# Two-layer encoder trunk on one core: weight loads run further ahead of the weight splits, and the splits queue behind ScalarE's other work

## The chip, the cores and the metric

The kernel runs on one core of a Trainium2 chip. The metric is the device time of one execution in microseconds, the median over several runs. Engines are named as in the profile: PE is TensorE (matmuls and transposes), PEld its weight loads, DVE is VectorE, ACT is ScalarE, POOL is GpSimd, SP is SyncE, which issues nearly all DMAs.

## What is computed

One sequence of 256 tokens with 2048 features passes two layers, all in float32. Each sub-layer is wrapped in RMS norms (one before, one after) and added to the residual `h`:

```python
for layer in range(2):
    hn = rms_norm(h, mix_pre_g[layer])
    y  = even(hn) if layer == 0 else odd(hn)      # attention, then its output projection
    h  = h + rms_norm(y, mix_post_g[layer])
    c  = memory_cross_attention(rms_norm(h, mem_pre_g[layer]), rms_norm(mem, mem_norm_g[layer]), wq, wk, wv, wo)
    h  = h + rms_norm(c, mem_post_g[layer])
    f  = relu(rms_norm(h, mlp_pre_g[layer]) @ w_up) ** 2 @ w_down     # 2048 -> 8192 -> 2048
    h  = h + rms_norm(f, mlp_post_g[layer])
```

`even` is 8 heads of 2-D neighbourhood attention and 8 heads of sliding-window attention with sinks; `odd` is differential attention with 8 heads of 256. Memory attention has 4 heads over 256 memory tokens.

## The kernel before

**Arithmetic.** Every float32 operand is split into a high and a low part in the `fp32r` format, and a product is three matmuls, high x high, high x low and low x high (`mm3`, line 257; the up projection of the MLP has its own loop, lines 721 and 725, where one matmul takes a high weight with both parts of the activation). PE therefore needs each weight in two parts, `w[:, 0]` and `w[:, 1]`.

**Weight units.** A unit is 256 rows by 512 columns of a weight matrix: 512 KB in HBM. `Weights.load` does all that a unit needs, at once in program order. SP issues the DMA into a raw buffer (line 180; three raw buffers). ACT writes the high part, DVE the low part. For input projections, where the norm's gain is folded in, these are two ACT instructions (line 193) and two DVE instructions (line 194) of 128x512; for output projections one of each, 128x1024 (lines 188 and 189). Nine buffers hold split units (`NW`); a few units use a buffer of another tile instead and may be loaded only when that is free (`gate`). PE asks for unit j by `W.get(j)`, and that call lets all units up to j + 4 be loaded (`AHEAD`). All units of the program stand in one list, in the order of use.

**Order of the work.** PE's order is written by hand: `manual_schedule` takes PE's instructions as the program issues them, and a small calendar (`Line`: `later`, `when`, `tick`, `until`) puts transposes and attention matmuls between the weight matmuls. ACT, DVE, POOL and SP are ordered by the compiler's scheduler, which follows the program order as a priority and takes what is ready. Each engine then runs its list strictly in order.

**The places that the prediction speaks of.** Blocks are 512 columns of a projection: 8 units, 96 matmuls of 128x512.

- `qs0` and `qs1`, the two blocks of sliding-window queries near the start. `evac_T` scales a finished block into a tile `q` on ACT (line 427), applies the rotary embedding on DVE (lines 412 to 415), has PE transpose it, and splits it into `qT` on ACT and DVE (lines 398 and 399).
- The memory queries (`mq`) and values (`mv`) in `mem_and_mlp`: `qT` is split in the same way, between units of `mv` and `mo`; the memory features `mt` come from DRAM and are split into `xT` (lines 340 and 341).
- The end of a sub-layer, `Leave` (lines 361 to 393). It takes the output projection in chunks of 512 columns, in the order token tile 0, chunks 0 to 3, then token tile 1. For each chunk DVE adds the matmul result into `y` (line 307), ACT takes the sum of squares (`junk`, line 321), DVE multiplies by the gain (line 375); after chunk 3 DVE forms `rb` (line 383), POOL takes the inverse root `rr` (line 325) and DVE updates the four blocks of `h` (line 388). PE transposes these blocks (line 348) between later matmuls, and ACT and DVE split them into `xT`.
- An MLP group is 512 of the 8192 hidden columns: 96 matmuls of the down projection of one group (line 257), then the up projection of a later one (lines 721 and 725). `split_u` brings its result out: `ue` on ACT (line 679), `s` on DVE, square and relu on ACT, then the split into `lt` (lines 398 and 399).

Of the kernel before, what the change touches and what calls it, by code (L numbers as in the profile page):

```python
# [3 lines left out]

# [1 line left out]

# [23 lines left out]
NW = 9  # L30
# [7 lines left out]
D_TRS, D_RMS, D_EVM, D_EVU, M_TR, M_GO = 4, 13, 11, 6, 11, 1  # L38
A_ROPE, A_NA, M_AT = 10, 1, 8
A_DF, DF_GAP, DF_T, DF_M, DF_O = 6, 5, 7, 4, 8  # L40
AHEAD = 4
L_MQ, L_MV, L_UP, L_Q = 6, 5, 8, 6
START = (2, 6, "AAAaABaBabbraBBabababbbab")
G_MIX, G_MEM, G_MLP, G_MN = 0, 2, 4, 6
# [27 lines left out]
def trunk(  # L72
# [3 lines left out]
    mlp_w_up, mlp_w_down, out,  # L76
):
    nc = tc.nc
    V, A, G, PE = nc.vector, nc.scalar, nc.gpsimd, nc.tensor
# [18 lines left out]
    gains = keep.tile([P, P], F32, name="gains")  # L98
# [24 lines left out]
    class Line:  # L123
        def __init__(self):
            self.now, self.q, self.n = 0, [], 0
# [21 lines left out]
        def until(self, done):  # L147
            while not done():
                self.now, _, fn = heapq.heappop(self.q)
                fn()  # L150

    line = Line()


    class Weights:
        def __init__(self):
            self.specs, self.tiles, self.n, self.wait, self.open = [], {}, 0, [], set()
            self.goal, self.live = -1, 0

        def plan_in(self, src, n0, g, spare=(), gate=None):  # L160

# [12 lines left out]
                    self.specs.append((src, k0 + 2 * kp, n * 512, None, None, None))  # L174
            return a

        def load(self, j):
            src, k0, n0, tag, _, g = self.specs[j]
            raw = rawp.tile([P, 2, 512], F32, tag="raw", name="raw")
            nc.sync.dma_start(  # L180
                raw, src[k0 * P : (k0 + 2) * P, n0 : n0 + 512].rearrange("(k p) n -> p k n", p=P)
            )
            if tag is None:
                w = wp.tile([P, 2, 2, 512], F32R, tag="w", name="w")
            else:
                w = sb.tile([P, 2, 2, 512], F32R, tag=tag, bufs=1, name="w")
            if g is None:
                A.copy(w[:, 0], raw)  # L188
                V.tensor_tensor(w[:, 1], raw, w[:, 0].bitcast(F32), ALU.subtract)  # L189
            else:  # L190
                for kk in range(2):
                    gk = gains[:, g * KT + k0 + kk : g * KT + k0 + kk + 1]
                    A.activation(w[:, 0, kk], raw[:, kk], AF.Copy, scale=gk)  # L193
                    V.scalar_tensor_tensor(  # L194
                        w[:, 1, kk], raw[:, kk], gk, w[:, 0, kk].bitcast(F32), ALU.mult, ALU.subtract
                    )
            self.tiles[j] = w

        def pump(self):
            while self.n < min(self.goal + 1, len(self.specs)):  # L200
                _, _, _, tag, g, _ = self.specs[self.n]
                if g is None or g in self.open:
                    if tag is None:
                        if self.live == NW:
                            return
                        self.live += 1
                    self.load(self.n)
                else:
                    self.wait.append(self.n)
                self.n += 1  # L210

        def upto(self, j):
            self.goal = max(self.goal, j)
            self.pump()

        def free(self, gate):

            self.open.add(gate)
            for j in self.wait:
                self.load(j)  # L220
            self.wait = []

        def get(self, j):
            self.upto(j + AHEAD)
            return self.tiles[j]

        def done(self, j):

            if self.specs[j][3] is not None:
                return  # L230

            self.live -= 1
            self.pump()

    W = Weights()
# [418 lines left out]
    def mem_and_mlp(l, R, kT, nxt):  # L654
# [31 lines left out]
        def up(g):  # L686
# [42 lines left out]
            for b in range(2):  # L729
                split_u(ut, 2 * b, pts[2 * b : 2 * b + 2])  # L730
# [4 lines left out]
        for g in range(NG):  # L735
# [249 lines left out]
```

## Time and profile before

| | us |
|---|---|
| median of 3 runs | 2377.68 (2373.12 to 2378.13) |
| the profiled execution's own time | 2374.78 |
| its span, first to last instruction | 2372.7 |
| PE busy in it | 2346.2 (99%) |
| DVE busy | 1611.9 (68%) |
| ACT busy | 1377.7 (58%) |
| mean DMA rate | 190 GB/s |
| mean granted TensorE clock | 0.998 of full speed |

The profiled execution took 2.1 us more than its span, for what lies before the first and after the last instruction, and it was 2.9 us under the median of the runs. Times in the trace count from the span's start. In the rows below, the idle time in brackets is that of the engine just before the instruction, with what ended it.

### The profile page before, as it was taken

The page shows a single profiled execution, that of the slowest core. Times are in us where ns is not written, and L with a number is a line of the kernel's source. Part 1 is how long each engine was busy: PE and PEld are TensorE (multiplying, and loading weights), DVE is VectorE, ACT ScalarE, POOL GpSimd, SP SyncE. Part 2 cuts the span into 40 slices and gives each one's busy share as a digit, 9 for nine tenths or more (in the row PEclk, how much of TensorE's full clock was granted, in tenths as well). Part 3 has the DMA queues.
Part 4 walks back from the last instruction along what each step waited for, and adds up shares of the span by engine and source line. Part 5 has one row for each costly group of instructions (what it writes and reads, how often), then busy time and mean ns, then how long its engine had stood idle before and what let it go on. Part 6 is the DMA issues. An engine that isn't in the chain of part 4 may idle for free.

```text
span 2372.7 us, 32033 instructions
## 1 busy us (share of the span) xinstructions
PE 2346.2 (99%) x11687; PEld 1984.9 (84%) x11687; DVE 1611.9 (68%) x2545; ACT 1377.7 (58%) x2280; POOL 28.0 (1%) x46
## 2 busy tenths in 40 slices
PE   8999999999999999999999999999999999999998
PEld 7788887888888888888888888887888888888887
DVE  6776678856666656666876667788666666666666
ACT  6756567765545545545665655577655545555553
POOL 0000000000000000000000000000000000000000
PEclk9999999999999999999999999999999999999999
DMA  7657655565655666665565555655666665665663
GB/s 250 212 183 233 188 193 190 178 209 181 198 193 183 195 196 183 195 197 187 180 195 172 171 188 169 204 178 181 202 195 194 187 195 187 188 199 182 196 195 114
DMA packets 238279, 451.88 MB, mean 190 GB/s; under 512 B 21289, under 2 KB 22185, under 8 KB 237353
## 3 DMA queue, kind: packets, MB, share of 16 engines
q1 hardware_dynamic: 237832, 449.32, 59.7%
q8 instruction: 91, 1.49, 0.3%
q14 instruction: 68, 0.55, 0.1%
q10 hardware_dynamic: 288, 0.52, 0.1%
HBM read 445.59 MB, written 5.15 MB: 190 GB/s over the span
## 4 chain that ended last, share of the span: by engine, by line
PE 91%; DMA 3%; DVE 3%; ACT 2%; issue 1%; POOL 0%; SPq 0%; DVEq 0%; POOLq 0%; ACTq 0%
PE mm L257 59%; PE at L721 14%; PE at L725 7%; PE mm L721 5%; PE mm L725 2%; PE at L257 2%; DVE w L194 1%; DMA raw<-in_even_w_in 1%; PE tr L435 1%; DMA raw<-in_odd_w_in 1%; PE tr L348 1%; ACT w L193 1%; PE at L505 0%; DMA h<-in_x 0%; ACT junk L321 0%
## 5 line engine op out<-in xcount | busy, mean ns | idle before, releaser
L257 PE MATMUL mm<-w,lt 128*128 128x512 f32 x4032 | 926.9, 390 | 0.0
L257 PEld LDWEIGHTS mm<-w,lt 128*128 128x128 f32 x4032 | 754.8, 188 | 155.9
L194 DVE SCALAR_TENSOR_TENSOR w<-raw,gains,w 128x512 fp32r<-128x512 f32 x944 | 678.2, 747 | 261.5 <-ACT w L193 258.7
L193 ACT ACTIVATE w<-raw,gains 128x512 fp32r<-128x512 f32 x944 | 636.0, 717 | 354.1 <-PE mm L257 268.9
L257 PE MATMUL mm<-w,xT 128*128 128x512 f32 x2784 | 674.0, 395 | 2.0 <-DVE v L403 1.1
L189 DVE TENSOR_TENSOR w<-raw,w 128x1024 fp32r<-128x1024 f32 x336 | 411.2, 1224 | 377.6 <-ACT w L188 376.8
L188 ACT CAST w<-raw 128x1024 fp32r<-128x1024 f32 x336 | 353.1, 1051 | 439.1 <-PE mm L725 193.3
L257 PEld LDWEIGHTS mm<-w,xT 128*128 128x128 f32 x2784 | 513.2, 189 | 104.4 <-DVE v L403 1.9
L721 PE MATMUL at<-xT,w 128*128 128x512 f32 x1440 | 368.8, 391 | 0.0
L721 PEld LDWEIGHTS at<-xT,w 128*128 128x128 f32 x1440 | 262.7, 188 | 49.0
L725 PE MATMUL at<-xT,w 128*128 128x256 f32 x1440 | 211.0, 283 | 0.0
L725 PEld LDWEIGHTS at<-xT,w 128*128 128x128 f32 x1440 | 197.2, 191 | 9.4
L312 DVE TENSOR_TENSOR y<-mm,y 128x512 f32<-128x512 f32 x256 | 175.5, 685 | 15.6 <-PE mm L257 15.4
L721 PE MATMUL mm<-xT,w 128*128 128x512 f32 x480 | 147.8, 389 | 0.0
L721 PEld LDWEIGHTS mm<-xT,w 128*128 128x128 f32 x480 | 90.1, 188 | 19.3
L725 PE MATMUL mm<-xT,w 128*128 128x256 f32 x480 | 96.7, 283 | 0.0
L725 PEld LDWEIGHTS mm<-xT,w 128*128 128x128 f32 x480 | 74.9, 192 | 0.0
L679 ACT COPY ue<-at 128x256 f32<-128x256 f32 x90 | 33.7, 374 | 28.0 <-DVE s L680 13.9
L399 DVE TENSOR_TENSOR lt<-s,lt 128x512 fp32r<-128x512 f32 x64 | 44.1, 689 | 3.6 <-ACT lt L398 3.6
L257 PEld LDWEIGHTS at<-kT,qT 128*128 128x128 f32 x240 | 34.5, 191 | 10.5 <-ACT qT L398 4.2
L257 PE MATMUL at<-kT,qT 128*128 128x256 f32 x240 | 37.3, 288 | 5.8 <-ACT qT L398 3.4
L321 ACT ACTIVATE junk<-y 128x512 bf16<-128x512 f32 x32 | 20.1, 629 | 38.5 <-DVE y L307 38.3
(113 smaller groups left out, 1063.6 us busy)
## 6 DMA issues: line engine op xcount, KB each, us to landing
raw<-in_mlp_w_up SPq DMA_DIRECT2D x256, 512.0 KB, 4.1
raw<-in_mlp_w_down SPq DMA_DIRECT2D x256, 512.0 KB, 4.2
raw<-in_odd_w_in SPq DMA_DIRECT2D x96, 512.0 KB, 4.2
raw<-in_even_w_in SPq DMA_DIRECT2D x72, 512.0 KB, 4.3
raw<-in_even_w_out SPq DMA_DIRECT2D x32, 512.0 KB, 4.2
raw<-in_odd_w_out SPq DMA_DIRECT2D x32, 512.0 KB, 3.8
mt<-memT SPq DMA_DIRECT2D x32, 256.0 KB, 4.0
raw<-in_mem_wk SPq DMA_DIRECT2D x16, 512.0 KB, 4.4
```

Source lines behind the costliest of these rows:

```text
L188: A.copy(w[:, 0], raw)
L189: V.tensor_tensor(w[:, 1], raw, w[:, 0].bitcast(F32), ALU.subtract)
L193: A.activation(w[:, 0, kk], raw[:, kk], AF.Copy, scale=gk)
L194: V.scalar_tensor_tensor(w[:, 1, kk], raw[:, kk], gk, w[:, 0, kk].bitcast(F32), ALU.mult, ALU.subtract)
L257: PE.matmul(pt, lhs(a), rhs(b), start=first and i == 0, stop=last and i == 2)
L312: V.tensor_tensor(ysl, pt, ysl, ALU.add)
L348: PE.transpose(pt[:, i * P : (i + 1) * P], h[:, t, k * P : (k + 1) * P], ident)
L399: V.tensor_tensor(lo, src, hi.bitcast(F32), ALU.subtract)
L435: PE.transpose(tp[:, i * P : (i + 1) * P], u[:, i * P : (i + 1) * P], ident)
L679: A.copy(e, pt[:, S:])
L721: PE.matmul(pts[nt], wn, both, start=kp + kk == 0, stop=kp == 7 and kk == 1)
L725: PE.matmul(pts[nt][:, :S], wn, both[:, :S], start=False, stop=False)
```

## The change

`Weights.load` is cut in two. `fetch(j)` takes a raw buffer and issues the DMA; `split()` takes the oldest raw buffer and issues the ACT and DVE instructions. `W.get(j)` now lets units up to j + 6 be fetched and units up to j + 4 be split, and there are four raw buffers in place of three. A small class `Urgent` stands in for ACT and notes the last instruction that anything but a weight split has issued there. The splits are issued under `tc.issue_after(A.last)`: each ACT instruction of a split gets an edge that keeps it behind that noted instruction in ACT's list. Units that wait for a gate go to a list `shut`, and when the gate opens to `late`, from which they are fetched first. The tile `ue` shares two buffers with `q` instead of having its own two, which makes room for the fourth raw buffer. The matmuls and their order are as before.

```diff
-AHEAD = 4
+AHEAD, FETCH, NRAW = 4, 2, 4
-    rawp = ctx.enter_context(tc.tile_pool(name="rawp", bufs=3))
+    rawp = ctx.enter_context(tc.tile_pool(name="rawp", bufs=NRAW))
+    class Urgent:
+        def __init__(self):
+            self.last = None
+        def activation(self, *a, **k):
+            self.last = nc.scalar.activation(*a, **k).ins
+        def copy(self, *a, **k):
+            self.last = nc.scalar.copy(*a, **k).ins
+    A = Urgent()
...
-        def load(self, j):
-            src, k0, n0, tag, _, g = self.specs[j]
+        def fetch(self, j):
+            src, k0, n0 = self.specs[j][:3]
             raw = rawp.tile([P, 2, 512], F32, tag="raw", name="raw")
             nc.sync.dma_start(
                 raw, src[k0 * P : (k0 + 2) * P, n0 : n0 + 512].rearrange("(k p) n -> p k n", p=P)
             )
+            self.raws.append((j, raw))
+
+        def split(self):
+            j, raw = self.raws.pop(0)
...
-            if g is None:
-                A.copy(w[:, 0], raw)
...
+            with tc.issue_after(A.last) if A.last is not None else nullcontext():
+                if g is None:
+                    nc.scalar.copy(w[:, 0], raw)
+                    V.tensor_tensor(w[:, 1], raw, w[:, 0].bitcast(F32), ALU.subtract)
+                else:
+                    for kk in range(2):
+                        gk = gains[:, g * KT + k0 + kk : g * KT + k0 + kk + 1]
+                        nc.scalar.activation(w[:, 0, kk], raw[:, kk], AF.Copy, scale=gk)
...
         def pump(self):
...
+            while True:
+                j = self.next()
+                if j < min(self.fetch_goal + 1, len(self.specs)) and len(self.raws) < NRAW:
+                    self.fetch(j)
...
+                elif self.raws and self.raws[0][0] <= self.split_goal and (
+                    self.live < NW or self.specs[self.raws[0][0]][3] is not None
+                ):
+                    self.split()
                 else:
-                    self.wait.append(self.n)
-                self.n += 1
+                    return
...
         def get(self, j):
-            self.upto(j + AHEAD)
+            self.upto(j + AHEAD, FETCH)
             return self.tiles[j]
...
-                e = sb.tile([P, S], F32, tag="ue", bufs=2, name="ue")
+                e = sb.tile([P, S], F32, tag="q", bufs=2, name="ue")
```

PE's list and POOL's list hold the same instructions in the same order before and after. The lists of ACT, DVE and SP are in another order; three places follow. Line numbers of the changed kernel lie some 17 to 35 higher than those of the kernel before: L162 and L165 are the noted ACT instructions, L210 and L215 the splits on ACT, L216 those on DVE.

ACT at the end of block `qs0`, before (`q_570` and `q_579` bring out the two halves of `qs0`; the `w` are weight units of `qs1`, of which `w_532` and `w_551` are the third and fourth):

```order
L193 ACTIVATE w_532<-raw_530,gains_88 128x512 x2
L193 ACTIVATE w_551<-raw_549,gains_88 128x512 x2
L427 ACTIVATE q_570<-mm_404,rs_568 128x512
L193 ACTIVATE w_591<-raw_589,gains_88 128x512 x2
L427 ACTIVATE q_579<-mm_418,rs_577 128x512
L193 ACTIVATE w_611<-raw_609,gains_88 128x512 x2
L193 ACTIVATE w_637<-raw_635,gains_88 128x512 x2
L398 CAST qT_403<-tr_628 128x512
```

The same place now (the first unit of `qs1` is `w_498`):

```order
L162 ACTIVATE q_574<-mm_408,rs_572 128x512
L162 ACTIVATE q_583<-mm_422,rs_581 128x512
L215 ACTIVATE w_498<-raw_453,gains_88 128x512 x2
L215 ACTIVATE w_517<-raw_477,gains_88 128x512 x2
L215 ACTIVATE w_536<-raw_496,gains_88 128x512 x2
L215 ACTIVATE w_555<-raw_515,gains_88 128x512 x2
L215 ACTIVATE w_595<-raw_534,gains_88 128x512 x2
L215 ACTIVATE w_615<-raw_553,gains_88 128x512 x2
L165 CAST qT_407<-tr_632 128x512
```

Both `q` of `qs0` now stand ahead of all splits for `qs1`; before, the first four units of `qs1` were split ahead of them.

DVE at the end of the MLP of layer 0, `Leave`, before (the matmul results `mm_10021`, `mm_10061` and `mm_10078` are the last chunk of token tile 0 and the first two of token tile 1):

```order
L307 TENSOR_TENSOR y_83<-mm_10021,y_83 128x512
L375 TENSOR_TENSOR y3_10051<-y_83,g_9928 128x512
L383 TENSOR_SCALAR rb_10053<-ssl_9930,part_9932 128x1
L388 SCALAR_TENSOR_TENSOR h_82<-y_83,rr_10055,h_82 128x512 x3
L388 SCALAR_TENSOR_TENSOR h_82<-y3_10051,rr_10055,h_82 128x512
L307 TENSOR_TENSOR y_83<-mm_10061,y_83 128x512
L194 SCALAR_TENSOR_TENSOR w_10179<-raw_10177,gains_88,w_10179 128x512
L307 TENSOR_TENSOR y_83<-mm_10078,y_83 128x512
```

The same place now (`mm_10025`, `mm_10065` and `mm_10082` are the same three chunks):

```order
L342 TENSOR_TENSOR y_83<-mm_10025,y_83 128x512
L342 TENSOR_TENSOR y_83<-mm_10065,y_83 128x512
L410 TENSOR_TENSOR y3_10055<-y_83,g_9932 128x512
L418 TENSOR_SCALAR rb_10057<-ssl_9934,part_9936 128x1
L342 TENSOR_TENSOR y_83<-mm_10082,y_83 128x512
L423 SCALAR_TENSOR_TENSOR h_82<-y_83,rr_10059,h_82 128x512 x3
L423 SCALAR_TENSOR_TENSOR h_82<-y3_10055,rr_10059,h_82 128x512
```

The four updates of `h` stood ahead of the next two chunks' additions; now they stand behind both.

ACT at the second half of the memory queries in layer 1, before (`qT_13928<-tr_14264` is the split that the attention scores wait for):

```order
L193 ACTIVATE w_14236<-raw_14234,gains_88 128x512 x2
L188 CAST w_14249<-raw_14247 128x1024
L340 CAST xT_84<-mt_14189 128x4x128
L398 CAST qT_13928<-tr_14264 128x512
L487 ACTIVATE p_14278,s_14283<-at_14271,nm_14281 128x256 x2
```

The same place now:

```order
L215 ACTIVATE w_14227<-raw_14199,gains_88 128x512 x2
L215 ACTIVATE w_14240<-raw_14212,gains_88 128x512 x2
L165 CAST qT_13932<-tr_14270 128x512
L210 CAST w_14253<-raw_14225 128x1024
L162 ACTIVATE p_14284,s_14289<-at_14277,nm_14287 128x256 x2
```

The 128x1024 split of the first unit of `mo` and a split of `mt` stood ahead of `qT`; now `qT` stands ahead of that unit, and the `mt` splits are done earlier. In layer 0 the corresponding unit `w_3777` still stands ahead of `qT`.

## Rows read from the trace of the kernel before

**Rows 1.** The page, part 1: busy time, share of the span, instructions

```profile
PE 2346.2 (99%) x11687; PEld 1984.9 (84%) x11687; DVE 1611.9 (68%) x2545; ACT 1377.7 (58%) x2280; POOL 28.0 (1%) x46
```

**Rows 2.** Two consecutive MLP groups: busy time, granted clock, DMA

```profile
762.49:806.52 44.03, 44.03 (x225) 37.70 (x225) 28.61 (x39) 23.42 (x35) 0.00 (x0) 1.00 0.62 191
806.52:850.55 44.03, 44.03 (x225) 37.70 (x225) 28.60 (x39) 23.41 (x35) 0.00 (x0) 1.00 0.61 191
```

**Rows 3.** Wait view of PE: us in total, times, longest us

```profile
PE at L257 <- ACT qT L398: 3.4, 3, 1.7
PE at L257 <- DVE qT L399: 2.4, 3, 1.0
...
PE mm L257 <- ACT q L427: 0.9, 1, 0.9
PE at L257 <- DVE pT L399: 0.9, 1, 0.9
PE at L257 <- DVE lt L399: 0.8, 2, 0.4
```

**Rows 4.** Timeline, end of block qs0: start, duration, engine, line, instruction

```profile
60.06 0.67 ACT L427 ACTIVATE q<-mm,rs 128x512 f32<-128x512 f32 x1
...
60.78 4.40 PE L257 MATMUL mm<-w,xT 128*128 128x512 f32 x18 [0.87 <-ACT q L427]
...
60.92 0.22 DVE L412 TENSOR_TENSOR rope<-q,cst 128x64 f32<-128x64 f32 x1
...
61.52 0.74 DVE L194 SCALAR_TENSOR_TENSOR w<-raw,gains,w 128x512 fp32r<-128x512 f32 x1
```

**Rows 5.** Timeline of DVE, end of the MLP of layer 0

```profile
1150.05 0.21 DVE L383 TENSOR_SCALAR rb<-ssl,part 128x1 f32<-128x1 f32 x1
1150.92 2.74 DVE L388 SCALAR_TENSOR_TENSOR h<-y,rr,h 128x512 f32<-128x512 f32 x4 [0.66 <-POOL rr L325]
...
1154.84 0.68 DVE L307 TENSOR_TENSOR y<-mm,y 128x512 f32<-128x512 f32 x1
1155.44 0.68 DVE L375 TENSOR_TENSOR y<-y,g 128x512 f32<-128x512 f32 x1
```

**Rows 6.** The page, part 5: busy us, mean ns, idle before

```profile
L193 ACT ACTIVATE w<-raw,gains 128x512 fp32r<-128x512 f32 x944 | 636.0, 717 | 354.1 <-PE mm L257 268.9
...
L679 ACT COPY ue<-at 128x256 f32<-128x256 f32 x90 | 33.7, 374 | 28.0 <-DVE s L680 13.9
...
L321 ACT ACTIVATE junk<-y 128x512 bf16<-128x512 f32 x32 | 20.1, 629 | 38.5 <-DVE y L307 38.3
```

**Rows 7.** Timeline of PE and POOL, memory queries of layer 0

```profile
369.53 0.60 PE L348 MATMUL tr<-cst,h 128*128 128x128 f32 x4
...
372.74 0.60 PE L348 MATMUL tr<-cst,h 128*128 128x128 f32 x4
...
370.08 0.99 POOL L325 TENSOR_TENSOR rr<-rb,mhalf 128x1 f32<-128x1 f32 x1 [13.01 <-DVE rb L383]
```

**Rows 8.** Timeline at qT in layer 0, and the window around it

```profile
400.18 1.05 ACT L188 CAST w<-raw 128x1024 fp32r<-128x1024 f32 x1 [1.95 <-DMA raw<-in_mem_wo]
...
402.28 0.51 PE L257 MATMUL at<-kT,qT 128*128 128x256 f32 x2 [1.66 <-ACT qT L398]
...
400.00:409.00 9.00, 6.39 (x27) 5.16 (x26) 5.33 (x11) 4.78 (x11) 0.00 (x0) 0.81 0.44 155
```

**Rows 9.** Timeline at qT in layer 1, and the window around it

```profile
1609.85 0.50 PE L257 MATMUL at<-kT,qT 128*128 128x256 f32 x2 [1.28 <-ACT qT L398]
...
1609.00:1618.00 9.00, 7.20 (x37) 6.09 (x38) 7.20 (x16) 4.83 (x12) 0.00 (x0) 1.00 0.51 164
```

**Rows 10.** DMA issues, first 130 us: count, KB each, us to landing

```profile
bias<-scr SPq DMA_DIRECT2D x4, 96.0 KB, 4.6
```

**Rows 11.** Timeline of one MLP group, PE and ACT

```profile
762.33 21.92 PE L257 MATMUL mm<-w,lt 128*128 128x512 f32 x96
...
767.60 0.60 ACT L398 CAST lt<-s 128x512 fp32r<-128x512 f32 x1
```

More of the change, by code (lines that the diff above doesn't have):

```diff
@@ L2 @@
 import math
-from contextlib import ExitStack
+from contextlib import ExitStack, nullcontext
 import numpy as np
@@ L78, in trunk @@
     nc = tc.nc
-    V, A, G, PE = nc.vector, nc.scalar, nc.gpsimd, nc.tensor
+    V, G, PE = nc.vector, nc.gpsimd, nc.tensor
     keep = ctx.enter_context(tc.tile_pool(name="keep", bufs=1))
@@ L152, in trunk @@
     line = Line()
+    class Urgent:
[6 more added lines that the diff above has]
+    A = Urgent()
     class Weights:
         def __init__(self):
-            self.specs, self.tiles, self.n, self.wait, self.open = [], {}, 0, [], set()
-            self.goal, self.live = -1, 0
+            self.specs, self.tiles, self.n, self.open = [], {}, 0, set()
+            self.shut, self.late, self.raws = [], [], []
+            self.fetch_goal, self.split_goal, self.live = -1, -1, 0
         def plan_in(self, src, n0, g, spare=(), gate=None):
@@ L182, in load @@
             )
+            self.raws.append((j, raw))
+        def split(self):
+            j, raw = self.raws.pop(0)
+            _, k0, _, tag, _, g = self.specs[j]
             if tag is None:
+                self.live += 1
                 w = wp.tile([P, 2, 2, 512], F32R, tag="w", name="w")
@@ L186, in load @@
                 w = sb.tile([P, 2, 2, 512], F32R, tag=tag, bufs=1, name="w")
-            if g is None:
-                A.copy(w[:, 0], raw)
[L189 to L196, printed above, removed]
@@ L197, in load @@
-            self.tiles[j] = w
-        def pump(self):
[L200 to L207, printed above, removed]
-                else:
-                    self.wait.append(self.n)
-                self.n += 1
@@ L212, in upto @@
-        def upto(self, j):
-            self.goal = max(self.goal, j)
+            with tc.issue_after(A.last) if A.last is not None else nullcontext():
[6 more added lines that the diff above has]
+                        nc.scalar.activation(w[:, 0, kk], raw[:, kk], AF.Copy, scale=gk)
+                        V.scalar_tensor_tensor(
+                            w[:, 1, kk], raw[:, kk], gk, w[:, 0, kk].bitcast(F32), ALU.mult, ALU.subtract
+                        )
@@ new lines, in split, with next @@
+            self.tiles[j] = w
+        def next(self):
+            if self.late:
+                return self.late[0]
+            while self.n < len(self.specs):
+                g = self.specs[self.n][4]
+                if g is None or g in self.open:
+                    return self.n
+                self.shut.append(self.n)
+                self.n += 1
+            return len(self.specs)
+        def pump(self):
+            while True:
+                j = self.next()
+                if j < min(self.fetch_goal + 1, len(self.specs)) and len(self.raws) < NRAW:
+                    self.fetch(j)
+                    if self.late:
+                        self.late.pop(0)
+                    else:
+                        self.n += 1
+                elif self.raws and self.raws[0][0] <= self.split_goal and (
+                    self.live < NW or self.specs[self.raws[0][0]][3] is not None
+                ):
+                    self.split()
+                else:
+                    return
@@ L214, in upto @@
+        def upto(self, j, more=0):
+            self.split_goal = max(self.split_goal, j)
+            self.fetch_goal = max(self.fetch_goal, j + more)
             self.pump()
@@ L218, in free @@
             self.open.add(gate)
-            for j in self.wait:
-                self.load(j)
-            self.wait = []
+            self.late, self.shut = self.late + self.shut, []
+            self.pump()
         def get(self, j):
-            self.upto(j + AHEAD)
+            self.upto(j + AHEAD, FETCH)
             return self.tiles[j]
         def done(self, j):
-            if self.specs[j][3] is not None:
-                return
-            self.live -= 1
+            if self.specs[j][3] is None:
+                self.live -= 1
             self.pump()
```

## The prediction

> **What bounds the kernel now.** I read the busy times first. PE is busy 99% of the span, no other engine over 70% except PE's own weight loads, 84% [rows 1]. Then one stage at a time, since a mean hides stages. The MLP is 32 groups and well over half of the span; two neighbouring groups take 44.03 us each, the same to the hundredth, with PE busy for all of it [rows 2]. A stage in which PE never stands has nothing to give to a change that only brings weights or results earlier. So the change can matter only where PE waits, and the wait view lists these places: `qT` on ACT 3.4 us and on DVE 2.4, `q` 0.9, `pT` 0.9, `lt` 0.8 [rows 3]. That is 8.4 us in all, in some ten places in the attention parts, and PE waits for no weight unit. What PE waits for is a result that stands in ACT's or DVE's list behind a weight split. This caps the gain at about 8 us, or 0.35%, before any new wait. About 0.2%, or 4.75 us, is what a measurement of this kernel can tell from no change.
>
> PE's order is unchanged, so each place can be judged alone: how long is the chain of ACT and DVE work from one matmul to the next one that needs its result, and how many matmuls cover it? The cover is counted at 21.92 us for 96 matmuls, 0.228 us each [rows 11].
>
> **What goes.**
>
> 1. *`qT` in layer 0.* ACT waited 1.95 us for a DMA from `mem_wo`, split that unit for 1.05 us from 400.18, and only then came `qT`; PE stood 1.66 us for its high part [rows 8], and up to 1.0 for the low part [rows 3]. The unit still stands ahead of `qT` in the new list, but its DMA is let go two units earlier. At most the wait of 1.95 goes, and at least nothing, since four other units now crowd ahead of it. I take half, -1.0.
> 2. *`qT` in layer 1.* PE stood 1.28 us [rows 9] and again up to 1.0 [rows 3]. The 128x1024 split now follows `qT`. Its 1.05 us [rows 8] and part of the `mt` split that stood there go; the cast and low part of `qT` itself still take longer than the three matmuls before them. -1.3, between -1.0 and -1.6.
> 3. *`pT`* near 92 us, -0.9, and the two waits for `lt`, -0.6 of 0.8 [rows 3]: each result stood behind one 128x1024 split that is now behind it.
> 4. The third pair of waits for `qT`, some 1.2 us near 68 us, stays: twelve split instructions now stand ahead of it, as the order of ACT at `qs0` shows. 0.
>
> Sum of what goes: -3.8.
>
> **What comes.** Here I walk through the new lists.
>
> 1. *First unit of `qs1`.* Its split is now behind both `q`. From the end of the last matmul of `qs0`: hand-over 0.1, `q` 0.67, four rotary steps that hold DVE from 60.92 to 61.52, 0.6, then the low part of the unit, 0.74 [rows 4]: 2.1 us. One matmul of 0.2 runs on the high part alone, so PE stands 1.9 us. The old wait of 0.87 for `q` [rows 4] goes. Net +1.0, between 0 (units split sooner than I read) and +1.9.
> 2. *End of the MLP of layer 0.* The first update of `h` now stands behind the addition that waits for the very last matmul before the transposes of `h`. An addition holds DVE 0.60 us (1154.84 to 1155.44), an update a quarter of 2.74, 0.69 [rows 5]. With 0.1 of hand-over PE stands 1.4. Before it did not, the updates began at 1150.92 and ended ahead of that matmul's result. +1.4, between 0 and +1.6.
> 3. *End of `o3` in layer 1.* The same order with one chunk between: 12 matmuls cover 2.7 us. Behind the addition stand two multiplications, so 3 x 0.60, small steps 0.2, half a weight unit 0.74, `rb` to the first `h` 0.87, and the update 0.69 [rows 4, 5]: 4.3. +1.6, between 0 and +2.2.
> 4. *End of `oa1` in layer 0.* The same, but lighter: 0.60 twice, 0.87, 0.69 and hand-overs, 2.9 against 2.7. +0.2, up to +0.8.
> 5. *Memory queries of layer 0.* The fifth unit's low part now stands on DVE behind all four updates of `h` of token tile 1, and these behind a sum of squares that stands on ACT behind an `mt` split. Chain: that split about 0.6 and `junk` 0.63 [rows 6], `rb` to `h` 0.87, updates 2.74 [rows 5], low part 0.74 [rows 4], 5.6 us. Cover: PE's period of four transposes and twelve matmuls is 3.21 us (369.53 to 372.74) [rows 7], and four more transposes and two matmuls add 0.8: 4.0. +1.6. POOL took 0.99 here [rows 7], a little more than 0.66 of idle time in rows 5, so up to +2.2; at least 0.
> 6. *SP's queue.* The loads of the attention bias now stand behind raw fetches that wait for a buffer. They take 4.6 us to land [rows 10], and an addition on DVE ahead of the second softmax waits for the first of them. I find about 1 us of lateness with other work behind it, and take +0.4, between 0 and +2.
> 7. The rest is nothing, by its cover. In an MLP group the second four units of the down projection are now split after `lt`. `lt` ended at 768.20, 5.9 us after the group's first matmul, with gain splits between its steps that now come later; a split of 1.05 on ACT and about 1.3 on DVE (twice half a unit) would end at 8.2. The fifth unit is needed after 48 matmuls, at 10.9 [rows 4, 8, 11]. The margin is 2.7 us; if it were gone, each group would pay what is missing. The fourth raw buffer adds no instruction; `ue` keeps two buffers.
>
> Sum of what comes: 1.0 + 1.4 + 1.6 + 0.2 + 1.6 + 0.4 = +6.2. Net +6.2 - 3.8 = +2.4. On the profiled execution's 2374.78 us that is 2377.2. The runs' median lies 2.9 higher, at 2377.68, so I forecast **2380.0**, no change that can be told.
>
> **Rivals.**
>
> - *Gains alone.* The scheduler's list is only an order; if DVE reaches the updates of `h` with time to spare, the new waits shrink to little and the old ones go. All of what goes, the clock in layer 0 with it (see below), is -3.8 - 1.7 = -5.5; with 0.5 of new waits, 2372.7, at the best 8.4 + 1.7 less, 2367.6. For it: PE's waits in rows 3 do stand behind splits. Against: the orders printed above, where the work ahead of `h` is counted. Chance 0.17, of which 0.14 falls below 2372.9.
> - *The clock falls at the new waits* (slower). After PE's waits at 402 us the granted clock averaged 0.81 over 400 to 409 [rows 8]: part of that stretch ran at the lower level, 1.2 GHz, the rest at 2.4. That is at most 0.19 x 9 = 1.7 us. After the waits at 1610 it stayed at 1.00 [rows 9]. Ahead of the fall PE had stood 1.66 us and then up to 1.0; where it held, 1.28 and up to 1.0. My new waits of 1.9, 1.4, 1.6 and 1.6 us are like the one place as much as like the other. If each of the four is like the first and costs 1.7 us, +6.8: 2380.0 + 6.8 = 2386.8; two of them are enough for over 0.2%. Chance 0.17. The Trainium skill's page "TensorE: Matmul & The Clock Gate", section "HAM oscillation — how this bites in real kernels", says that a long enough stop between bursts of matmuls sends the next burst off at the lower clock, and that this is paid at every such stop. The row at 402 agrees, the row at 1610 shows a stop that was not long enough.
> - *The MLP margin is less than I count* (slower). Thirty of the groups bring `ue` out, 90 copies at three each [rows 6]. For each us beyond the margin of 2.7 the kernel takes 30 us more, 2410. Rows 11 speak against it. Chance 0.04.
> - *PE is not at its limit.* If matmuls could follow each other more closely once their data is early, the weight loads' 84% [rows 1] would be the measure, and 0.16 x 2373 = 380 us would be open; a fiftieth of it would be -7.6, 2370. Two groups of exactly 44.03 us with no wait in them [rows 2] say that nothing is open there. Chance 0.02. This is the rule of the Trainium skill's page "Perfetto Trace Analysis", section "Identifying the Most-Contended Engine": the busy share of matmuls is a poor measure of headroom, the busy share of weight loads a better one. The repeated 44.03 disagrees with it here.
>
> **How the numbers follow.** My own case has 0.60: from 2373.9 (the new waits at their lower bounds, -3.8) to 2384.6 (all at their upper ones, 10.7 - 3.8 = +6.9); 0.50 of it lies within 0.2% of the median, 0.10 above. Faster: 0.14 + 0.02 = 0.16. Slower: 0.10 + 0.17 + 0.04 = 0.31. Same: 0.50 + 0.03 = 0.53. The range reaches into the gains and takes in the clock: 2370.5 to 2389.0. It leaves out the MLP, and the far ends of the gains and of the clock.
>
> **What would show it.** Right: waits of 1 to 2 us for DVE `h` at transposes near 1153 and 1565 us, for a weight unit near 61 and 374 us, and no wait for `pT` near 92; ACT no longer idle for `mem_wo` near 400; an MLP group still at 44.03. Wrong: no wait at transposes of `h` (gains alone), a clock under 1.00 after the new waits, or a group longer than 44.1.

## The result and the profile after

The changed kernel took 2396.14 us, the median of 4 runs (2393.26 to 2399.3). The kernel before, run on the same chip, took 2375.72 (4 runs). The ratio is 1.0086, 95% interval [1.0067, 1.0106]. That is 20.4 us more, where 2380.0 with a range of 2370.5 to 2389.0 was forecast. The profiled execution took 2397.52 us, span 2395.7, against 2374.78 and 2372.7 before: the span grew by 23.0 us.

The page's first part, for the changed kernel:

```profile
PE 2355.3 (98%) x11687; PEld 1989.8 (83%) x11687; DVE 1595.7 (67%) x2545; ACT 1362.0 (57%) x2280; POOL 27.8 (1%) x46
```

No instruction was added [rows 1]. PE has 9.1 us more of busy time for the same matmuls, and the other 13.9 us of the 23.0 are time in which it stands. ACT and DVE show some 16 us less of busy time each, but they do not work faster: a gain split takes 716 ns on ACT where it took 717 [rows 6]. The busy time counts the overlap of neighbouring instructions once (944 gain splits of 717 ns are 677 us, and [rows 6] has 636.0 us), so less of it means that they stand closer together, in bunches. The wait view of PE says for what it stands (us in total, times, longest):

```profile
PE tr L383 <- DVE h L423: 5.8, 3, 2.9
PE at L610 <- DMA graw<-in_mem_norm_g: 5.7, 1, 5.7
PE at L292 <- ACT qT L165: 4.8, 4, 2.2
PE mm L292 <- ACT w L215: 4.0, 2, 2.6
PE mm L292 <- DVE w L216: 2.6, 4, 1.6
PE tr L733 <- ACT junk L162: 2.6, 2, 1.4
PE at L292 <- DVE qT L434: 1.7, 4, 0.6
```

The row with `graw` is the start of the program and was there before. Without the waits for a DMA at the start, all rows of this view, the smaller ones too, sum to 24.4 us, those of before to 10.4. So 14.0 us are waits. There are three new kinds: for `h`, for weight units (`w`), and at the transposes of `u` (L733), which stand behind `junk` on ACT at the start of the MLP. The old ones for `qT` grew in sum, from 5.8 to 6.5 us: near 68 us and in layer 0 they grew, in layer 1 they shrank from 2.24 to 0.54.

The remainder, PE's longer busy time, is mostly TensorE's clock. The window view gives busy time of PE, PEld, DVE, ACT, POOL, then the granted clock, the DMA share and GB/s:

```profile
60.00:80.00 20.00, 16.23 (x69) 12.50 (x70) 15.57 (x33) 11.54 (x22) 0.00 (x0) 0.91 0.64 200
409.00:420.00 11.00, 8.17 (x27) 6.62 (x27) 7.06 (x15) 4.50 (x11) 0.00 (x0) 0.69 0.56 196
720.00:764.00 44.00, 44.00 (x226) 37.67 (x225) 28.19 (x38) 23.43 (x34) 0.00 (x0) 1.00 0.57 192
1166.00:1176.00 10.00, 9.60 (x36) 7.78 (x37) 6.55 (x13) 2.14 (x6) 0.00 (x0) 0.68 0.11 40
1620.00:1635.00 15.00, 11.75 (x50) 8.90 (x49) 10.55 (x16) 9.24 (x15) 0.00 (x0) 0.89 0.56 191
```

In the four stretches outside the MLP the clock is at its full level of 2.4 GHz for a part only and at 1.2 GHz for the rest. A missing 0.31 of 11 us is at most 3.4 us, 0.32 of 10 is 3.2, 0.11 of 15 is 1.7 and 0.09 of 20 is 1.8: at most 10.1 us, where in the kernel before I found one such stretch, with at most 1.7 [rows 8]. With the waits, 14.0 + 8.4 = 22.4 of 23.0 us. The window in the MLP shows PE busy for all of it at full clock, as in [rows 2]: nothing changed there.

**The largest wait**, at the end of the MLP of layer 0. The timeline of the changed kernel (start, duration, engine, line, instruction; in brackets the idle time before it):

```profile
1157.72 5.83 PE L292 MATMUL mm<-w,lt 128*128 128x512 f32 x25
1160.15 0.74 DVE L216 SCALAR_TENSOR_TENSOR w<-raw,gains,w 128x512 fp32r<-128x512 f32 x1
...
1160.94 2.07 DVE L216 SCALAR_TENSOR_TENSOR w<-raw,gains,w 128x512 fp32r<-128x512 f32 x3
1162.92 1.28 DVE L342 TENSOR_TENSOR y<-mm,y 128x512 f32<-128x512 f32 x2
...
1164.84 0.69 DVE L342 TENSOR_TENSOR y<-mm,y 128x512 f32<-128x512 f32 x1
...
1165.59 2.74 DVE L423 SCALAR_TENSOR_TENSOR h<-y,rr,h 128x512 f32<-128x512 f32 x4
...
1166.40 1.11 PE L383 MATMUL tr<-cst,h 128*128 128x128 f32 x4 [2.85 <-DVE h L423]
```

Four low parts of the next block's weights hold DVE from 1160.15 to 1162.92. Only then come two additions, and a third at 1164.84, for the last matmul before the transposes; PE had ended that matmul at 1163.55. The updates of `h` stand behind all three. In [rows 5] `rb` and `h` stood first. The weights that went ahead here are not needed by the transposes that PE stands at.

**A wait of the edge's own making**, at the memory values of layer 1:

```profile
1619.74 1.27 ACT L165 CAST xT<-mt 128x512 fp32r<-128x512 f32 x2 [1.30 <-DMA mt<-memT]
...
1624.00 0.62 ACT L165 CAST xT<-mt 128x512 fp32r<-128x512 f32 x1 [2.41 <-DMA mt<-memT]
...
1624.97 0.62 ACT L165 CAST xT<-mt 128x512 fp32r<-128x512 f32 x1 [0.36 <-DMA mt<-memT]
1625.50 5.01 ACT L215 ACTIVATE w<-raw,gains 128x512 fp32r<-128x512 f32 x8
...
1626.27 0.64 PE L292 MATMUL mm<-w,xT 128*128 128x512 f32 x1 [2.56 <-ACT w L215]
```

ACT stands 2.41 us and again 0.36 for `mt`, and behind it stand eight split instructions which PE needs. The edge has put them behind the casts of `mt`, so ACT may not do them while it waits.

### The profile page after: what moved, and what is told of

It reads as the page before. It is cut to its first block, busy times and chain, and to the rows that moved or that the text cites. A ratio compares the mean times of both kernels' runs of the same rounds, so it can differ in the third digit from the quotient of the medians.

```text
span 2395.7 us, 31841 instructions
## 1 busy us (share of the span) xinstructions
PE 2355.3 (98%) x11687; PEld 1989.8 (83%) x11687; DVE 1595.7 (67%) x2545; ACT 1362.0 (57%) x2280; POOL 27.8 (1%) x46
## 4 chain that ended last, share of the span: by engine, by line
PE 88%; DVE 5%; DMA 3%; ACT 2%; issue 1%; POOL 0%; SPq 0%; DVEq 0%; POOLq 0%; ACTq 0%
PE mm L292 56%; PE at L756 14%; PE at L760 7%; PE mm L756 5%; PE mm L760 2%; PE at L292 2%; DVE w L216 2%; DMA mt<-memT 1%; ACT w L215 1%; DVE xT L376 1%; DVE h L423 1%; PE tr L470 1%; ACT junk L162 1%; PE at L540 0%; DMA h<-in_x 0%
## 5 line engine op out<-in xcount | busy, mean ns | idle before, releaser
L216 DVE SCALAR_TENSOR_TENSOR w<-raw,gains,w 128x512 fp32r<-128x512 f32 x944 | 660.1, 748 | 109.3 <-ACT w L215 106.2
L215 ACT ACTIVATE w<-raw,gains 128x512 fp32r<-128x512 f32 x944 | 620.2, 716 | 191.6 <-DMA raw<-in_mlp_w_up 136.9
L211 DVE TENSOR_TENSOR w<-raw,w 128x1024 fp32r<-128x1024 f32 x336 | 403.6, 1222 | 116.5 <-ACT w L210 114.1
L210 ACT CAST w<-raw 128x1024 fp32r<-128x1024 f32 x336 | 341.3, 1049 | 128.5 <-DMA raw<-in_mlp_w_down 92.4
L715 DVE TENSOR_TENSOR s<-at,ue 128x256 f32<-128x256 f32 x90 | 38.3, 425 | 297.9 <-ACT ue L165 295.7
L165 ACT COPY ue<-at 128x256 f32<-128x256 f32 x90 | 33.6, 373 | 326.6 <-PE at L756 321.3
L162 ACT ACTIVATE s<-s 128x512 f32<-128x512 f32 x120 | 74.6, 632 | 0.9
```

The source lines that it names most:

```text
L162: self.last = nc.scalar.activation(*a, **k).ins
L165: self.last = nc.scalar.copy(*a, **k).ins
L210: nc.scalar.copy(w[:, 0], raw)
L215: nc.scalar.activation(w[:, 0, kk], raw[:, kk], AF.Copy, scale=gk)
L216: V.scalar_tensor_tensor(w[:, 1, kk], raw[:, kk], gk, w[:, 0, kk].bitcast(F32), ALU.mult, ALU.subtract)
```

## The experiments

Each kernel was compared with the kernel before on the same chip (2374.7 to 2375.7 us, its medians), and each profile quoted is of one execution. In the expectations, E names the edge as the cause (E1 at the `mt` casts, E2 at the ends of sub-layers), F the longer queue of fetches on SP, L the lateness of the splits, G the place in the list that the fourth buffer gives to splits, and H its rival. What a text says beside a letter goes before this list.

### Which part of the change

**e1**, the changed kernel without its edge:

```diff
-            with tc.issue_after(A.last) if A.last is not None else nullcontext():
+            with nullcontext():
```

> The changed kernel with the edge taken out: splits are issued without issue_after, the rest of the change (fetch six ahead, four raw buffers, ue in the buffers of q) stays. Theory E (the edge makes the loss: splits wait in ACT's list for work that itself waits, and reach DVE in a bunch ahead of the updates of h): 2374 to 2379 us, the waits for h near 1166 and for a weight unit near 1626 gone. Theory F (the deeper fetch makes it: SP's list holds other loads behind raw fetches that wait for a buffer): 2390 to 2397, the wait near 1626 stays.

2381.66 us, ratio 1.0025 [1.0016, 1.0035], 2.7 above the range of theory E and far from F; both waits that it named are gone. The edge makes 14.5 of the 20.4 us. Six are left.

**e2**, the edge alone: `AHEAD, FETCH, NRAW = 4, 0, 3`, and `ue` with its own two buffers.

> The changed kernel with the edge alone: fetch and split both four ahead, three raw buffers, ue with buffers of its own. Theory E: 2390 to 2398 us, with the waits for h at the ends of the sub-layers as in the changed kernel. Theory F: 2374 to 2380, those waits gone.

2408.34 us, 1.0138 [1.0124, 1.0152], above both ranges. The edge costs 33 us with three raw buffers; the earlier fetch and the fourth buffer, which cost 6 without it, give 12 back with it. The parts do not add. (This kernel also has `load` cut in two. That was not run with three buffers and no edge; with four, e1 has it and e3 has not, and they lie 0.5 us apart.) The wait view of PE has more of the same kind:

```profile
PE tr L383 <- DVE h L423: 12.3, 5, 6.1
```

ACT's wait view shows one thing more, here for the changed kernel and for e2:

```profile
ACT w L215 <- DMA raw<-in_mlp_w_up: 136.9, 145, 2.3
ACT w L215 <- DMA raw<-in_mlp_w_up: 193.8, 189, 3.4
```

In the kernel before ACT stood 43.8 us for these loads, in e1 1.7. A unit whose split is held back keeps its raw buffer, so the next load is issued later, and ACT then stands for it. With three buffers in place of four there is less to take this up, which fits the 12 us; no run separates it from the order on DVE. In the MLP itself PE does not stand for it.

**e3**, the kernel before with a fourth raw buffer and nothing else (`bufs=4`, `ue` in `q`'s buffers to make room).

> The kernel before with a fourth raw buffer and ue in the buffers of q, nothing else. Both theories: within 3 us of the kernel before, 2373 to 2379. If the fourth buffer alone lets ACT reach the splits at qT sooner, the waits for qT near 402 and 1610 shrink and it is 2371 to 2374.

2381.20 us, 1.0024 [1.0013, 1.0035]: the six us of e1 come with the buffer alone. A buffer that adds no instruction was expected to be free. Its two largest waits of PE are those of e1 too (3.5 and 3.0 us there):

```profile
PE at L257 <- DVE v L403: 3.4, 2, 1.7
PE at L505 <- DVE p L524: 3.1, 1, 3.1
```

The waits for `qT` did shrink, from 5.8 to 2.1 us in all, and yet the kernel became slower: other places took their turn.

### Undoing the edge in one place

**e4**, the `mt` loads issued from POOL (`nc.gpsimd.dma_start`) and not from SP.

> The changed kernel with the loads of mt issued from POOL in place of SP. Theory F: the waits behind late mt go, 3.6 us near 1626 and what hangs on them, 2386 to 2392. Theory E: the edge still puts the splits behind the mt splits, but these no longer wait for a late load near 1626, so at most 4 us less, 2391 to 2396, with the waits for h as they were.

2400.32 us, 1.0108 [1.0094, 1.0121], above both ranges. The wait stayed, 3.38 us. So SP's queue is not what delays `mt`: there are two buffers for it, each load waits until DVE is done with the one before, and the cast of the new one started 3.6 us after the load was issued (POOL's load at 1621.97, the cast at 1625.52).

**e5**, the `mt` casts are not noted as ACT's last instruction, so splits need not stay behind them:

```diff
+        last = A.last
         split_x(t, n, d)
+        A.last = last
```

> The changed kernel, but the casts of mt into xT are not noted, so splits need not queue behind them. Theory E1 (near 1626 ready splits stand behind casts that wait for a load, and the load for one of two mt buffers): the wait for a weight unit near 1626 goes, 3.6 us and the clock after it, 2389 to 2393. Rival (the units themselves come late, whatever stands ahead of them): the wait stays, 2395 to 2397.

2390.72 us, 1.0065 [1.0052, 1.0077]: 5.4 us back, as theory E1 has it, and the wait near 1626 is gone. Its ACT timeline shows a split where ACT stood idle:

```profile
1613.58 1.30 ACT L165 CAST xT<-mt 128x512 fp32r<-128x512 f32 x2 [2.27 <-DMA mt<-memT]
...
1615.36 2.56 ACT L215 ACTIVATE w<-raw,gains 128x512 fp32r<-128x512 f32 x4
...
1621.77 1.03 ACT L210 CAST w<-raw 128x1024 fp32r<-128x1024 f32 x1
1622.71 0.57 ACT L165 CAST qT<-tr 128x512 fp32r<-128x512 f32 x1
```

The last two rows show the price: the first unit of `mo` stands ahead of `qT` again, and PE waits 1.61 and 0.88 us there, where it had waited 0.32 and 0.22. So this place alone does not give 5.4 us. Compared matmul by matmul, e5's profile gains 7.6 us on the changed kernel's: 1.7 between 1586 and 1697 us, around this place, 2.2 at the same place of layer 0, 1.0 ahead of it, and 2.7 between 1166 and 1197. There PE stops for `h` as long as before, 2.87 us, but the clock does not fall. That last part is nothing that the edit aimed at. How the 5.4 us of the medians are made up is not settled, and that they lie in the range of E1 may in part be luck.

**e6**, no edge in the last, staggered output blocks (`W.edge = not stagger` around them), which puts `h` on DVE back to its place of before.

> The changed kernel with the edge off while the last output projection of a sub-layer runs, where DVE's list then has the updates of h ahead of the next two chunks' additions again. Theory E2 (the order of DVE's list there makes the waits at the transposes of h): the waits near 365, 1166 and 1586 go, 6.3 us, and with them the fall of the clock after 1166, some 3 us: 2384 to 2389. Rival (splits arrive in a bunch from the blocks ahead, and DVE is late whatever its order): at most half of it goes, 2391 to 2396.

2398.62 us, 1.0104 [1.0088, 1.012]: no gain, and above both ranges. The wait for `h` near 365 us is gone, that near 1166 falls from 2.85 to 1.68 and that near 1586 from 2.13 to 0.32, but a wait of 2.62 for a weight unit appears near 407, and one of 1.5 for `v` in each memory attention.

**e7**, e5 and e6 together.

> Both of the last two edits. If E1 and E2 hold and the places are apart, the gains add up: 2378 to 2384, near the kernel without any edge (2381.7), of which only the rest of the fetch ahead remains as a loss. If one place takes over the other's wait: 2385 to 2392.

2395.19 us, 1.0084 [1.007, 1.0097]: a miss, and worse than e5 alone. The waits move on:

```profile
PE at L293 <- DVE v L441: 3.4, 2, 1.7
```

**e8**, the edge for output projections only, outside the last blocks; no earlier fetch, three raw buffers (`and g is None and self.edge`).

> Fetch and split both four ahead, three raw buffers, and the edge only for output projection units outside the last block of a sub-layer: those are the 128x1024 splits that stood ahead of pT, qT and lt in the kernel before. If a split that is ready should only stand back where a result for PE is about to be ready: waits for pT near 92, lt near 427 and 1632 gone, that for qT near 1610 down by 1.5: 2370 to 2374, faster than the kernel before. If the edge costs wherever it is: 2378 to 2386.

2408.66 us, 1.0136 [1.0121, 1.0152]: the clearest miss. The largest waits are three for `v` in layer 1's own attention:

```profile
PE mm L293 <- DVE v L441: 10.2, 3, 4.8
```

ACT's timeline ahead of the first of them:

```profile
1338.07 1.33 ACT L216 ACTIVATE w<-raw,gains 128x512 fp32r<-128x512 f32 x2 [1.56 <-DMA raw<-in_odd_w_in]
1339.31 1.24 ACT L162 ACTIVATE v<-mm,rr 128x512 fp32r<-128x512 f32 x2
```

No held 128x1024 cast is near. `v` stands behind a split of an input projection, which has no edge here, and ACT has stood 1.56 us for that split's load; at the third of them it stands for `mt`. ACT's waits for the loads of `in_odd_w_in` are 48.9 us in this run, 14.9 in the kernel before. So it is late loads that this run shows, as in e2; what makes them late was not tested by itself.

**e9**, two units more of lead: `AHEAD, FETCH, NRAW = 6, 2, 4`.

> The changed kernel with splits six and fetches eight units ahead, in place of four and six. Theory L (with the edge each split is issued later than before, so units and results come just in time everywhere, and more lead gives it back): 2378 to 2387 us, the waits for units near 60, 380 and 1626 gone. Theory B (the edge makes splits come in bunches whatever the lead, and DVE works through them ahead of what PE waits for): 2392 to 2402, with waits for h and for v as before or longer.

2391.73 us, 1.0076 [1.0064, 1.0089]: 4.4 back, between the two ranges. The waits for units near 60, 380 and 1626 are gone, but one of 1.29 came near 68, and those for `qT` grew (3.2 and 2.8 us near 410 and 1624). Lateness of the splits is a part of the loss only.

**e12**, the same edge on DVE too: low parts behind DVE's latest other instruction.

> The changed kernel with the same edge on DVE too: low parts queue behind DVE's latest other work issued so far. Theory B: if low parts ahead of additions and updates on DVE make the waits, some of them go, 2384 to 2392. Theory L: the low parts come later still, 2396 to 2410.

2399.36 us, 1.0108 [1.0095, 1.0122]: 3 us more than the change. Later low parts do not help.

### The fourth buffer, and single edges

**e11**, e1 with the loads of the attention bias from POOL, to see whether their place on SP's list makes the wait of 3.0 us for `p` near 80 us.

> The kernel without any edge (fetch six ahead, four raw buffers), with the loads of the attention bias issued from POOL in place of SP. Theory F (what the fetch ahead costs there is the 3.2 us at the second transposes of the softmax near 82, where DVE's addition to the bias waits for a load that stands in SP's list behind raw fetches): 2377 to 2379.5, 3 us under 2381.7. Rival (the loads land late because of the traffic, not the list): 2380.5 to 2383.

2378.57 us, 1.0018 [1.0009, 1.0027]. 3 us less than e1, in theory F's range but not by its reason: the wait for `p` was still 2.4 us. The bias was not its cause; where the 3 us came from is not settled. DVE's timeline of **e3** shows what is:

```profile
76.06 1.22 DVE L189 TENSOR_TENSOR w<-raw,w 128x1024 fp32r<-128x1024 f32 x1
77.20 0.15 DVE L494 TENSOR_TENSOR s<-s,e 128x2 f32<-128x2 f32 x1
...
77.56 1.23 DVE L189 TENSOR_TENSOR w<-raw,w 128x1024 fp32r<-128x1024 f32 x1
...
78.78 1.21 DVE L189 TENSOR_TENSOR w<-raw,w 128x1024 fp32r<-128x1024 f32 x1
79.90 0.61 DVE L524 TENSOR_SCALAR p<-p,r 128x256 f32<-128x256 f32 x2
```

Three low parts of units of `os0`, 3.6 us, stand between the steps of the first head's softmax: the fourth buffer let these units in sooner, and the scheduler took them as soon as they were ready. PE stood 3.06 us for `p`. The same at the last half of `v` in both memory attentions, where the eighth unit of `mo` had slipped ahead.

**e13** tests just that: e3 with edges at these three places.

```diff
+            if not MARK:
+                for k in range(3):
+                    MARK["d", U["os0"] + k] = i_
...
+            if unit is not None and t == NT - 1:
+                MARK["a", unit], MARK["d", unit] = i
...
+                with behind(("a", j)):
+                    A.copy(w[:, 0], raw)
+                with behind(("d", j)):
+                    V.tensor_tensor(w[:, 1], raw, w[:, 0].bitcast(F32), ALU.subtract)
```

`i_` is the division of `p` of the first head; `unit` is the eighth unit of `mo`, `i` the two instructions that bring out the last half of `v`; `behind` is `issue_after` on what is marked.

> The kernel before with the fourth raw buffer (2381.2 us when run alone so, 6 over before) and edges at three places only: on DVE the low parts of the first three units of os0 stand behind the first head's p (its division by the sum), and the eighth unit of mo is split behind the last half of v, on ACT and on DVE, in both layers. Theory G (the buffer lets units be split sooner, the scheduler places them ahead of softmax and v, and that is the whole cost): the wait of 3.2 us near 80 us goes and the two of 1.88 near 428 and 1635 fall to 0.6 or less, 2381.2 - 3.2 - 2.6 = 2375.4, between 2374 and 2377. Theory H (the cost lies elsewhere, or the waits move to the next place as they did when the general edge was undone in one place): 2379.5 or more.

2373.50 us, 0.9994 [0.9985, 1.0003]: all of the six us gone, and 7.7 below e3, a little more than the 5.8 expected. The wait for `p` is gone and the two for `v` are 0.28 us each. The profile of e3 also has three falls of the clock, near 65, 80 and 425 us, that of e13 only the first. The same place in e13:

```profile
77.23 0.17 DVE L505 RECIPROCAL r<-s 128x2 f32<-128x2 f32 x1
77.43 0.62 DVE L533 TENSOR_SCALAR p<-p,r 128x256 f32<-128x256 f32 x2
77.96 1.22 DVE L196 TENSOR_TENSOR w<-raw,w 128x1024 fp32r<-128x1024 f32 x1
```

`p` is done 2.5 us sooner, and the low part after it is in nobody's way. So the buffer itself costs nothing that can be told; the order that followed from it did.

**e10**, the kernel before with one edge in each layer: the first unit of `mo` is split behind the second `qT` (a unit held back until that cast is issued, then split behind it).

```diff
+        W.hold = U["mo", l]
+        in_block(U["mq", l], evac_T(qT, R, q=True, ev=D_EVM, then=W.release), lag=L_MQ, between=between)
```

> The kernel before with one edge: the first unit of mo in each layer is split behind the second qT, and nothing else is moved. If the single split that stands ahead of qT costs what the wait view says: 2.0 us near 402 and 1.7 near 1610, with the clock after 402 staying full another 1.2: 2369.5 to 2373. If the softmax behind it becomes the wait, since two splits now stand ahead of its first exponential: 2374 to 2378.

2372.10 us, 0.9993 [0.9984, 1.0002]; 2.7 us below the kernel before, too little to tell from no change. In its profile the waits at `qT` of layer 0 are shorter than in [rows 8], and the clock did not fall, which may or may not be due to the edge (see the last section):

```profile
402.20 0.51 PE L263 MATMUL at<-kT,qT 128*128 128x256 f32 x2 [1.13 <-ACT qT L404]
```

```profile
400.00:409.00 9.00, 7.53 (x43) 6.29 (x42) 6.22 (x14) 5.49 (x13) 0.00 (x0) 1.00 0.50 170
```

**e14**, e10 and e13 together.

> The run before with the edge at the first unit of mo as well, in both layers, which alone took 2.7 us off the kernel before. Theory G: the gains add, 2375.4 - 2.7 = 2372.7, between 2370.5 and 2375, qT waits of 1.3 us in each layer. Theory H: 2377 or more.

2374.87 us, 0.9998 [0.999, 1.0007], inside the range of theory G, but no better than e13. PE's two waits at `qT` sum to 1.3 us in each layer, as expected. In e13 they were 1.6 and 0.6 already: there the first unit of `mo` of layer 0 is split at 397.75, 4.1 us ahead of PE's transposes of `q`, and is out of the way. The edge at `mo` had next to nothing left to take away.

No version tried is faster than the kernel before by more than its measurement can tell.

## Why the prediction was wrong

**What held.** The MLP margin was enough: PE is busy for all of the window at 720 to 764. `pT` near 92 us and the two `lt` no longer wait, 1.7 us where 1.5 was forecast (what goes, step 3). `qT` in layer 1 gave 1.7 where 1.3 was (step 2). The new waits stand where the walk through the lists put them: for `h` near 1166 and 1586, and for a unit near 60 and 380. Two rivals are out, gains alone and PE not at its limit: both would have been faster. The list of PE's waits that capped the gain at 8.4 us had left out 2.0 us of the same view, 1.7 for `v` and 0.3 for `q`; the forecast did not use them, but `v` is where the fourth buffer cost time in e3.

**Step 1 of what comes** (first unit of `qs1`, +1.0) was right in kind. PE stands 1.44 us for the high part and 0.60 for the low one, together 2.0, where 1.9 was worked out.

**Step 2 of what comes** (end of the MLP, +1.4, at most 1.6) took the place in the list for the whole delay. It counted the addition and the update from the moment that the matmul result is there, as if DVE came to the addition on time. It came 1.29 us late, 1164.84 after 1163.55, since the four low parts in the timeline above had pushed the additions before it. PE stood 2.85 us. **Step 3** (end of `o3`, +1.6) was right in kind: PE stood 2.13, inside its range. **Step 4** (+0.2, up to 0.8) became 0.85 near 365 us. **Step 6** (+0.4) came to nothing: PE has no wait near the second softmax.

**Step 5** (memory queries of layer 0, +1.6) came as worked out, 1.56 us near 380. But I looked at one layer. In layer 1 PE stood 2.56 us near 1626, by another mechanism, a stand of ACT for `mt` with the splits behind it, which no step had.

**Step 1 of what goes** (`qT` of layer 0, -1.0) failed. The first unit of `mo` still stood ahead of `qT`, and its load came later, not earlier:

```profile
402.58 1.26 ACT L165 CAST xT<-mt 128x512 fp32r<-128x512 f32 x2 [2.37 <-DMA mt<-memT]
403.75 5.01 ACT L215 ACTIVATE w<-raw,gains 128x512 fp32r<-128x512 f32 x8
...
406.11 6.35 SPq L195 DMA_DIRECT2D raw<-in_mem_wo  x5
...
409.76 1.05 ACT L210 CAST w<-raw 128x1024 fp32r<-128x1024 f32 x1 [1.01 <-DMA raw<-in_mem_wo]
410.72 0.58 ACT L165 CAST qT<-tr 128x512 fp32r<-128x512 f32 x1
...
411.35 0.79 PE L292 MATMUL at<-kT,qT 128*128 128x256 f32 x2 [2.25 <-ACT qT L165]
```

ACT's idle time fell from 1.95 [rows 8] to 1.01 us, the half that I took. But everything ahead was later too, and PE's wait grew from 1.66 to 2.25. The step let the load go two units earlier. A load needs a free raw buffer, and here all four held units whose splits stood behind the casts of `mt`, for which ACT stood 2.37 us. The load was issued at 406.11, 2.0 us ahead of PE's transposes of `q` at 408.15; in the kernel before it was issued at 394.94, 4.7 ahead of those at 399.66.

**Step 4 of what goes** (`qT` near 68 us, taken to stay) was wrong too. PE stood 0.91 us there before; now it stands 0.84, 0.47, 1.40 and 0.46, 3.17 us in all, since ACT stands for the loads of the next units with `qT` behind their splits. The fall of the clock at 60 to 80 us comes after these stops:

```profile
72.32 0.50 PE L292 MATMUL at<-kT,qT 128*128 128x256 f32 x2 [1.40 <-ACT qT L165]
```

**The clock rival** (+6.8 for four such places, chance 0.17) came true beside my own case and not in its place. My own case took the clock at nothing; it cost up to 8.4 us more than before. Stops near 72, 411, 1166 and 1626 went with a clock of 0.91, 0.69, 0.68 and 0.89 over the stretches above. The rival priced one fall at 1.7 us; two cost up to 3.4 and 3.2. Its reason holds in part only: after the new stops of 1.56 us near 380 and 2.13 near 1586 the clock stayed at 1.00. The Trainium skill's page "TensorE: Matmul & The Clock Gate", section "HAM oscillation — how this bites in real kernels", says that a long enough stop between bursts of matmuls sends the next burst off at the lower clock. The rows at 411 and 1166, with stops of 2.25 and 2.85 us, agree; a stop of 2.87 us at the same place in e5 was followed by 1.00 (last section), so the length of a stop did not decide here; the measurement stands against the rule.

**Step 7 of what comes** (the rest is nothing, by its cover) is the one wrong in principle. Some 7 us of new waits lie where no step looked: 2.7 at a unit of `mv` in layer 1, 2.6 at the transposes of `u` in two places, 0.9 for `rb` near 1197, 0.5 for `xT` near 390 and 0.3 for a unit near 405. And of its words "the fourth raw buffer adds no instruction" only the words are right: in e3 the buffer alone cost 6 us, and e13 shows through which instructions.

So the sum failed in step 7, in the clock that it took at nothing, and in step 4 of what goes and step 2 of what comes, and it failed in its form. The edge costs 33 us alone (e2), 14.5 beside the earlier fetch (e1), and undoing it at one kind of place brought 5.4 us (e5), at another nothing (e6, 2398.62), and at both together 1.0 (e7). These parts interact, since each split that moves pushes another. I added places as if each stood alone. How the 14.5 us are shared among the places stays open. For the wait near 1626 e5 settles the cause, the edge behind the casts of `mt`, but not its share.

## What to carry to other kernels

On an engine that runs its list strictly in order, an edge "behind everything issued so far" moves work behind instructions that are not ready yet, and the engine then stands with ready work in hand (2.41 us for `mt` here). Put an edge only at a wait that a trace shows, from the one instruction that is in the way to the one that is late: e13 did so at three places and took 7.7 us off e3, where the general edge added 14.5. Work held back also holds its staging buffer, and with it the next load. And an undone wait should be looked for again further on: in e6 and e7 the time that one place gave back was lost at the next. A deeper prefetch can slow a kernel without adding an instruction, because ready work is scheduled sooner, also ahead of work on the critical path; after adding a buffer, look at the order around the softmax steps.

## What the runs showed of the hardware that was not expected

A stop of PE can cost more than its length, and its length alone does not tell whether it does. In the changed kernel a stop of 2.85 us near 1166 was followed by a granted clock of 0.68 over the next 10 us, which is up to 3.2 us besides. In e5 the same transposes come after a stop of 2.87 us:

```profile
1163.18 0.66 PE L383 MATMUL tr<-cst,h 128*128 128x128 f32 x4 [2.87 <-DVE h L423]
```

```profile
1163.00:1173.00 10.00, 9.82 (x50) 8.18 (x51) 9.18 (x18) 4.74 (x12) 0.55 (x1) 1.00 0.15 46
```

The clock did not fall, nor did it in e4 after 2.86 us. Shorter stops do the same both ways: after 1.30 and 0.29 us near 65 the clock over 65 to 75 was 0.83 in e3 and 1.00 in e1. In e10 it stayed at 1.00 over 400 to 409 after stops of 1.13 and 0.34 us, where the kernel before with 1.66 and 0.95 had 0.81 [rows 8]; by the runs above, that can't be put down to the shorter stop. So a wait in this kernel has two prices, its length, and its length and up to 1.8 or 3.4 us more, and one profile shows only one of them. Waits are therefore better compared by their length, and times by the median of several runs. What decides between the two prices is not shown here.
